# 44 adaLN pieces in the recurrence and the later ones in twos, in a hybrid RWKV-7 / RG-LRU trunk on one core

## The chip, the core and the metric

The kernel runs on one NeuronCore of a Trainium2 chip. A core has five engines with instruction queues of their own: TensorE (PE, matmuls into PSUM), VectorE (DVE), ScalarE (ACT), GpSimd (POOL) and SyncE (SP), which here issues nearly all transfers. The metric is device time in microseconds of one launch, the median of several runs.

## What is computed

One inference step of a two-layer trunk, width 2048, for a prompt of 256 rows and 8 single-row samples with carried state. Layer 0 mixes with RWKV-7, layer 1 with an RG-LRU; each mixer is followed by a causal ConvFFN of width 5632. The vectors that shift, scale and gate each stage (adaLN) come from the conditioning `c` through `w_mod`.

```python
mod = (silu(c) @ w_mod[i] + b_mod[i]).reshape(B, 6, 1, D)     # 2048 x 12288 for each layer
sh_m, sc_m, gt_m, sh_f, sc_f, gt_f = [mod[:, j] for j in range(6)]
h = rms_norm(x, g0) * (1 + sc_m) + sh_m
out = mixer(h)                       # RWKV-7: r, k, v, decay; scan over 256 rows of a 64 x 64 state, 32 heads
x = x + gt_m * rms_norm(out, g1)
h = rms_norm(x, g2) * (1 + sc_f) + sh_f
x = x + gt_f * rms_norm(conv_ffn(h), g3)
```

The scan is `S = S * d + (S a) b^T + v k^T`, `y = S r`, row by row; the outputs are `x` and all new states.

## The kernel before, in words

The work runs in stages: projections r, k, v (to about 395 us), the recurrence (to 763 us), the output projection of layer 0 (to about 875 us), the first ConvFFN (to about 1728 us), the RG-LRU (to about 2079 us), the second ConvFFN (to the end).

*Weights.* All large weights stream from `in_wst` as tiles of 128 x 2048 floats (1 MB), two groups of weights to a tile (class `Stream`, line 407). A group is split on ScalarE (`wh`, line 434) and VectorE (`wl`, line 435) into a high and a low half, and `mm_pieces` (448) spends 24 matmuls of 264 columns on it. `mm_group` (461) runs the groups of one set of four output tiles and asks for weights two tiles ahead.

*adaLN pieces.* `w_mod` beyond what the projections need comes as 160 pieces of 1 MB (`in_wmr`), 16 to a vector; a piece is four matmuls of 512 columns, each into 32 columns of the array (`wm_mm`, 342; the trace has 8 records to a piece). `wm_load` (372) loads one, `wm_pump` (377) computes the next in turn, and with `ahead` also loads the one behind it. The last piece of a vector is followed by a transposition and `mod_fin`. `mod` (399) hands out a vector and computes at once what is missing of it. `residual_and_h` (550) runs four pieces at its start (561), while the norm is waited for.

*Tiles.* Weights and pieces share five tiles of 1 MB in turn (`raw_tile`, 367): NRAW = 2 named `raw`, which live through the whole kernel, and three named `rawx`, of pools that are closed before the recurrence and opened behind it (lines 658, 871, 1426). In the recurrence there are only the `raw` tiles.

*The recurrence.* 16 pairs of heads go through jobs that are generators: load, prep, diag, solve, levels, prepb, seq (the scan by chunks of 64 rows), out, and the sample's own steps. The order in which their steps are written to the engines' queues is the table ORDER (37): `3p2` is three steps of prep for pair 2. `w` is a step of `pump_load` (1394), one half of a piece's transfer, and `u` is `pump_step` (1400), its matmuls. NPUMP = 60 pieces are done there; engines run in program order, with no reordering by the scheduler (line 1415). Elsewhere the tile scheduler orders the queues.

*Behind it.* `pace[0] = PACE` (1485) turns on a piece behind every fifth group of weights in `mm_group`. `out_proj` (1469) runs three sets of eight groups (the first set is written out above it), and in its first set the callback `bg_x` (1487) loads x back into U0 in four parts.

Of the kernel before, what the change touches and what calls it, by code (L numbers as in the profile page):

```python
# [38 lines left out]
l3 w1 p2 d0 3p2 4p1 a1 2b0 d1 b0 2b1 3g0 3p2 b1 p2 l5 p2 3p3 l3 2p3 2b0 d0 d1 s0 p3 w1 2p3 u0 u1 2p2 s2 3p3  # L39
5b1 p4 p3 2l4 g0 2p4 p5 s0 2p5 p4 3g0 l5 p5 w2 s0 w2 w3 2g0 p2 w3 g0 l6 p2 d2 p3 g0 5p2 6p3 d3 u2 u3 2g0 s0  # L40
3p4 2b2 w4 p4 3p5 b2 b1 4p4 b1 2p5 2b2 g0 s0 3b2 d2 d3 w4 2s2 5g0 p5 w5 3g0 2p4 u4 3p4 l7 p4 3b3 p5 2s2 s0 p5
2b3 g0 2b2 w5 u5 3b3 g0 p5 2w6 2p5 p4 2p5 p6 q0 2p6 2a0 2p5 u6 2a0 2q0 l6 s0 v0 b3 p6 2a0 5p6 b3 p6 s2 a0 p6
a0 3v0 2p7 a0 4h0 l8 l9 p7 l7 p7 d5 d4 l8 w7 2h0 3p7 4p8 v1 p7 v1 h0 2v1 l9 2p7 2v0 h0 p7 2p9 h0 p9 v1 s2 v1
p9 3v0 2v1 v0 v1 d4 d5 v1 2a1 p7 v0 q0 p6 w7 u7 2w8 u8 3s4 2a1 3q0 s2 2v2 q0 v1 w10 v2 3q0 p7 a1 p7 3q0 p7 2w9
v2 p6 l10 2q0 2p6 q0 2p6 s4 q0 2p6 a1 3p7 v3 3q0 v3 a0 s4 2a1 w10 v2 2p8 q0 2o0 q0 v3 v2 3b4 p8 a1 u9 u10 a1
p7 2p8 d6 3p8 l10 a2 p10 v3 o0 3p10 b5 o0 a2 q1 v3 2q1 d7 q1 2w11 o0 d6 q1 v3 s4 2a2 v2 d7 s4 v2 a2 a3 v2 w12
q0 2o0 s6 2p8 d8 2q1 v2 2o0 p8 a2 s4 3q1 o0 v2 p8 p9 s6 q1 l12 2q1 2a2 d8 q1 v3 q1 2p8 2a2 2p9 v3 4o0 3v3 3v4
q1 v4 3b4 a3 a2 b4 p8 b4 p9 3a3 w12 u11 u12 p9 v4 b4 3q1 2v4 a4 v4 b4 4q1 3a3 v4 h0 2s6 2w13 3p9 2b5 2p10 2b5
p10 2w14 b6 a3 2l11 3b5 a3 2v4 p10 p11 q1 a4 u13 u14 a3 2w15 b5 2o1 2w16 s6 a5 b5 3p9 p10 2q2 2a4 p9 q2 p9 d9
v5 2o1 a4 o1 2p11 2p9 o1 2v5 o1 s6 p11 s6 2q2 o1 u15 3q2 2w17 a4 2o1 a4 b7 d9 s8 3q2 2v5 a4 v5 2q2 a4 3q2 u16  # L50
4q2 s6 2w18 v5 q2 b6 p11 2q2 2p11 3v5 p11 3o2 3v6 3p10 v5 o1 b6 2p12 u17 u18 q3 p12 q3 a4 l12 p12 v6 a5 3p10
2q3 2l13 2b6 q3 o1 a4 q3 2b6 2w19 v6 2o2 w20 v6 s8 q3 a5 q3 p10 2q3 b6 q2 2o2 2p10 a5 w20 2a5 3v6 a6 u19 u20
p10 l14 o2 4q3 4a5 d10 2o2 w21 4q3 2v6 a5 2b6 q3 w21 2q3 p12 b7 q3 2p12 b7 o3 o2 o3 q4 s8 u21 d10 2o1 w22 2o2
w22 w23 u22 q4 q3 4p11 3q4 o2 p11 2a6 2q4 3p11 b8 4q4 2p11 2v7 w23 u23 2w24 2v7 d11 p13 2v7 a7 3p13 q3 p11 2q4
u24 2w25 w26 5q4 p12 w26 3v7 4s8 3q4 2a6 d11 2o3 l14 2q4 o4 p12 2v7 o3 u25 2o4 p12 2q5 2p12 q4 3a6 p12 2q5 w27
s10 w27 2a6 p12 d12 2p12 2b8 s14 a7 3p13 p12 a7 s8 4p14 2o3 q5 o3 o4 p13 u26 u27 q5 2p12 o4 v8 2l15 2o3 3v8 o3
d12 3q5 2b7 a7 2b7 3q5 2b8 q5 2a7 b8 4q5 b7 2w28 u28 o4 2p14 w29 b7 o3 q5 2o4 a7 b7 v8 b8 w29 o4 v8 o4 u29 3b8
v8 2q5 o4 a6 2a7 2w30 2v8 2s10 2o3 q5 v8 2q5 p13 v9 o5 2w31 a7 3p13 u30 a8 a7 u31 v8 o5 o4 5b9 a8 q6 a8 q5
2p13 3q6 a8 q6 2p13 2s10 b10 s10 p13 2b9 3a8 2w32 u32 q6 p15 2p14 p15 p14 p15 2w33 3o5 q6 p15 2w34 s10 d13 2q6
2o4 q6 u33 q6 w35 2q6 w35 b9 a8 v9 3q6 v9 2p13 v9 q6 2a8 2b9 q6 d13 2q6 v9 o5 2q6 p15 v9 o6 2p15 q6 a9 p15 o6  # L60
u34 u35 q7 o5 a8 p14 q7 2o5 2w36 w37 2p14 3q7 2o5 s10 p14 a9 p14 d14 p14 w37 4q7 v9 u36 w38 2v9 3a9 q7 p15 2v9
2a9 4q7 2b10 3q7 s12 4b10 w38 4q7 s12 2p14 3a9 2q7 a9 v10 u37 u38 a10 v11 2s12 v10 2p15 s12 p15 b11 p15 2v10
2p15 2w39 2p15 a11 4b11 v10 2b11 2v11 v10 2a10 3v10 v11 q6 q7 u39 2o6 s12 2o7 q8 d15 v10 4q8 v10 2w40 u40 2w41
2q8 a10 o5 s12 2o6 a10 2o6 o5 u41 5q8 w42 o5 w42 o6 2q8 o6 q8 o7 o6 o7 q8 u42 o7 p14 w43 q8 a10 2q8 a10 w43
3a10 v11 3q8 o8 q8 w44 o6 w44 o8 q9 v11 2o6 o7 4q9 2o8 2o7 q9 2a11 p14 a11 q9 u43 u44 d14 d15 o7 s12 v12 2q9
w45 o7 q9 w45 o8 2w46 o8 v12 4q9 3o8 2q9 o7 u45 3q9 v12 2w47 v12 o8 2v12 4q9 2o9 2s14 q10 o7 a11 2o7 o9 q10
s14 2q10 a10 q8 q10 2o9 b10 u46 2o8 3o9 2w48 u47 q10 b10 o9 q10 o9 b10 2q10 2b12 2q10 b12 3b11 4o9 o8 u48 2q10
b12 2q10 o8 q10 2b12 2w49 q9 b12 2a11 b12 2a11 q10 b13 3q10 2w50 b13 2q10 2s14 q10 2b12 2o10 u49 u50 a12 o10
q10 2o10 6b13 2a11 b14 w51 2b14 w51 4b14 a12 o10 u51 4o10 v13 2w53 2b13 3v11 3v12 a12 b14 3a12 v13 2p15 2v13
a12 2v11 v12 w52 v13 w52 q11 v13 u52 u53 2q11 v12 3a12 3q11 2a13 2b14 q11 v13 q11 s14 q11 v13 b15 q11 s14 q11  # L70
2v14 v13 a12 2o10 v14 w54 v14 v13 4a13 v14 w54 a13 v13 v14 w55 q11 w55 q11 u54 5q11 o10 3a13 q11 a13 2q11 b15
2q11 o10 2o11 q12 u55 2o11 q12 b15 2q12 o11 b15 v15 2q12 b15 2q12 2a14 b15 q12 2b15 a14 q12 2o11 2v15 4q12 v15
2o11 2w56 a14 q12 o11 3q12 q11 2v15 2a14 2q12 2b15 2q12 2o12 a14 q13 2q12 u56 2o11 2o12 o11 a14 2o12 o11 3q13
3o12 2q13 w57 o12 2a14 2q13 3o12 2q13 v14 2q13 o12 v14 2q13 v15 v14 q13 w59 2v15 2v14 a15 q13 4a15 2q13 2a15
w57 u57 3q13 a15 3q13 2o13 q14 v15 3q14 a15 v15 5q14 a15 3q14 o13 e0 o13 a15 10q14 o14 e0 o14 q14 4q15 o13
4q15 w58 6q15 o14 q15 e0 q15 w58 6q15 u58 e0 2o13 q15 2e0 q14 o14 o15 o14 e0 w59 u59 o15 2o13 2o14 4o13 o14
o13 6o14 a14 q15
# [1714 lines left out]
```

## Time and profile before

| | |
|---|---|
| median of 3 runs | 2910.57 us (2909.17 to 2916.7) |
| the profiled execution | 2907.63 us |
| its span, first to last instruction | 2905.9 us |
| TensorE busy | 2786.0 us, 96% |
| VectorE, ScalarE, GpSimd busy | 1756.3, 1366.6, 511.6 us |
| mean granted TensorE clock | 0.983 |
| moved by DMA | 648.48 MB, mean 223 GB/s |

The profile is one execution. Busy times are sums over stages with different limits, so the stretch of a stage is read for itself. Names of tiles are the program's, numbers of buffers are left out, and `L345` is line 345 of the kernel before; the changed kernel's lines are one less there.

### The profile page before, as it was taken

The page shows a single profiled execution, that of the slowest core. Times are in us where ns is not written, and L with a number is a line of the kernel's source. Part 1 is how long each engine was busy: PE and PEld are TensorE (multiplying, and loading weights), DVE is VectorE, ACT ScalarE, POOL GpSimd, SP SyncE. Part 2 cuts the span into 40 slices and gives each one's busy share as a digit, 9 for nine tenths or more (in the row PEclk, how much of TensorE's full clock was granted, in tenths as well). Part 3 has the DMA queues.
Part 4 walks back from the last instruction along what each step waited for, and adds up shares of the span by engine and source line. Part 5 has one row for each costly group of instructions (what it writes and reads, how often), then busy time and mean ns, then how long its engine had stood idle before and what let it go on. Part 6 is the DMA issues. An engine that isn't in the chain of part 4 may idle for free.

```text
span 2905.9 us, 61725 instructions
## 1 busy us (share of the span) xinstructions
PE 2786.0 (96%) x25868; PEld 2529.8 (87%) x25868; DVE 1756.3 (60%) x2830; ACT 1366.6 (47%) x2195; POOL 511.6 (18%) x1044
## 2 busy tenths in 40 slices
...
GB/s 329 285 264 257 171 162 230 286 269 250 209 248 214 234 242 229 235 234 231 233 235 229 242 258 188 220 231 221 261 221 236 231 176 181 182 177 186 174 188 77
DMA packets 148438, 648.48 MB, mean 223 GB/s; under 512 B 41360, under 2 KB 60960, under 8 KB 81600
## 3 DMA queue, kind: packets, MB, share of 16 engines
...
## 4 chain that ended last, share of the span: by engine, by line
PE 74%; DMA 4%; DVE 3%; ACT 2%; issue 1%; SPq 0%; POOL 0%; DVEq 0%; ACTq 0%; POOLq 0%
PE bk L455 16%; PE bk L456 15%; PE bk L457 15%; PE sq L455 6%; PE sq L456 6%; PE sq L457 6%; PE wm L345 5%; DMA raw<-in_wmr 3%; PE bk L895 1%; DVE bt L545 1%; ACT wh L434 0%; PE bk L901 0%; DVE U L546 0%; PE bk L582 0%; PE bk L1231 0%
## 5 line engine op out<-in xcount | busy, mean ns | idle before, releaser
L435 DVE TENSOR_TENSOR wl<-rawx,wh 128x1024 fp32r<-128x1024 f32 x460 | 565.4, 1231 | 488.2 <-ACT wh L434 468.5
L434 ACT CAST wh<-rawx 128x1024 fp32r<-128x1024 f32 x460 | 481.1, 1048 | 663.2 <-PE bk L456 454.2
L455 PE MATMUL bk<-AH,wh 128*128 128x264 f32 x2352 | 672.7, 286 | 0.0
L457 PE MATMUL bk<-AH,wl 128*128 128x264 f32 x2352 | 668.7, 284 | 0.2 <-DVE wl L435 0.2
L456 PE MATMUL bk<-AL,wh 128*128 128x264 f32 x2352 | 668.8, 284 | 0.0
L435 DVE TENSOR_TENSOR wl<-raw,wh 128x1024 fp32r<-128x1024 f32 x300 | 369.3, 1233 | 329.8 <-ACT wh L434 323.3
L455 PE MATMUL bk<-ah,wh 128*128 128x264 f32 x1822 | 525.7, 289 | 8.0 <-ACT ah L488 5.5
L457 PE MATMUL bk<-ah,wl 128*128 128x264 f32 x1822 | 520.8, 286 | 0.5 <-DVE wl L435 0.5
L456 PE MATMUL bk<-al,wh 128*128 128x264 f32 x1822 | 520.8, 286 | 0.0
L434 ACT CAST wh<-raw 128x1024 fp32r<-128x1024 f32 x300 | 313.7, 1048 | 434.8 <-PE bk L456 285.0
L455 PEld LDWEIGHTS bk<-AH,wh 128*128 128x128 f32 x2352 | 443.4, 189 | 34.4 <-issue 29.3
L456 PEld LDWEIGHTS bk<-AL,wh 128*128 128x128 f32 x2352 | 442.7, 188 | 0.2 <-DVE AL L489 0.2
L457 PEld LDWEIGHTS bk<-AH,wl 128*128 128x128 f32 x2352 | 441.8, 188 | 0.4 <-DVE wl L435 0.4
L455 PEld LDWEIGHTS bk<-ah,wh 128*128 128x128 f32 x1822 | 344.2, 189 | 33.9 <-issue 21.6
L457 PEld LDWEIGHTS bk<-ah,wl 128*128 128x128 f32 x1822 | 344.6, 189 | 1.4 <-DVE wl L435 0.8
L456 PEld LDWEIGHTS bk<-al,wh 128*128 128x128 f32 x1822 | 344.7, 189 | 0.6 <-DVE al L489 0.2
L455 PE MATMUL sq<-AH,wh 128*128 128x264 f32 x1040 | 297.3, 286 | 0.0
L456 PE MATMUL sq<-AL,wh 128*128 128x264 f32 x1040 | 295.7, 284 | 0.0
L457 PE MATMUL sq<-AH,wl 128*128 128x264 f32 x1040 | 295.4, 284 | 0.0
L1525 POOL COPY fgs<-gt 128x10 f32<-128x10 f32 x88 | 49.4, 585 | 1306.8 <-ACT gt L1519 1285.6
L455 PEld LDWEIGHTS sq<-AH,wh 128*128 128x128 f32 x1040 | 196.0, 189 | 15.2 <-issue 13.4
L456 PEld LDWEIGHTS sq<-AL,wh 128*128 128x128 f32 x1040 | 195.7, 188 | 0.0
...
## 6 DMA issues: line engine op xcount, KB each, us to landing
rawx<-in_wst SPq DMA_DIRECT2D x233, 1024.0 KB, 4.8
raw<-in_wst SPq DMA_DIRECT2D x151, 1024.0 KB, 4.9
raw<-in_wmr SPq DMA_DIRECT2D x120, 512.0 KB, 6.0
rawx<-in_wmr SPq DMA_DIRECT2D x57, 1024.0 KB, 6.5
raw<-in_wmr SPq DMA_DIRECT2D x43, 1024.0 KB, 5.1
rawx<-in_wmq SPq DMA_DIRECT2D x18, 1024.0 KB, 5.8
raw<-in_wmq SPq DMA_DIRECT2D x14, 1024.0 KB
...
```

The costliest lines, as they stand in the source:

```text
L345: PE.matmul(ps[32 * g:32 * g + 32, :cols], cs[:, k0 + kk, :], raw[:, (kk * 4 + g) * cols:(kk * 4 + g + 1) * cols], start=(k0 + kk == 0), s ...
L434: S.copy(wh, t)
L435: V.tensor_sub(wl, t, wh.bitcast(F32))
L455: PE.matmul(ps[:, :n], h[:, kk, sl], xh, start=first and kk == 0, stop=False)
L456: PE.matmul(ps[:, :n], h[:, kk, sl], xl, start=False, stop=False)
L457: PE.matmul(ps[:, :n], l[:, kk, sl], xh, start=False, stop=last and kk == 1)
L545: e.tensor_tensor(t, U1[:, j:j + n, :TP], r1[:, None, :TP].to_broadcast([128, n, TP]), op=mult)
L895: PE.matmul(out[HH[(i + turn) % 2]], lhs[HH[i]], rhs[HH[i]], start=start, stop=stop, skip_group_check=True)
L1525: G.tensor_copy(gs[:, m], gt[:, TP:])
```

## The change

PACE is 4 in place of 5, NRAW 3 in place of 2 (so three `raw` and two `rawx` tiles), NPUMP 44 in place of 60, and ORDER is another table: the same jobs for the 16 pairs, 16 `u` and 32 `w` fewer, in another order throughout. Behind the recurrence pieces come in twos: of each eight groups of weights, loads are written behind the fourth and fifth, and two pieces are computed behind the eighth, without loading ahead. The two loads ahead of a residual stage move from the fifth to the last group of their set. `bg_x` now runs over two sets of groups and loads a part of x at the second and seventh group of each.

```diff
-PACE = 5
-NRAW = 2
+PACE = 4
+NRAW = 3
-NPUMP = 60
+NPUMP = 44
 ORDER = """
-p0 s0 h0 g0 l0 p0 l0 3p0 g0 3p0 2l1 4p1 4p0 2g0 4p1 g0 3p1 p0 p1 b0 a0 4p0 l2 2p0 p2 b0 l2 2b0 2p1 w0 p1 b0 w0
+p0 p1 2g0 2l0 2p0 l1 p1 p0 s0 l1 p0 g0 3p0 l2 4p0 p1 l3 2p0 2w0 5p1 2p0 4p1 p2 3p0 p2 2g0 p3 p2 l2 p2 3p1 3b0
...
@@ mm_group
             if bg is not None:
                 bg(q)
-            if q == 4 and ahead:
+            pace[1] += 1
+            if pace[0]:
+                p = pace[1] % (2 * pace[0])
+                if p in (PACE, PACE + 1):
+                    wm_load(wm_state["i"] + p - PACE)
+                elif p == 0:
+                    wm_pump(2, False)
+            if ahead and q == nk // 2 - 1:
                 for w in range(ahead):
                     wm_load(wm_state["i"] + w)
-            pace[1] += 1
-            if pace[0] and pace[1] % pace[0] == 0:
-                wm_pump(1)
@@ out_proj
-            pss = pss0 if g == 0 and pss0 else mm_group(16, rhs, bg if g == bg0 else None, 2 if g == 3 else 0)
+            bgg = (lambda q: bg(q + 8 * (g - bg0))) if bg0 <= g < bg0 + 2 else None
+            pss = pss0 if g == 0 and pss0 else mm_group(16, rhs, bgg, 2 if g == 3 else 0)
@@ bg_x
-        if q in (3, 4, 5, 6):
-            SP.dma_start(U0[:, 4 * q - 12:4 * q - 8, 1:], I["xT"][:, 4 * q - 12:4 * q - 8])
+        if q % 8 in (1, 6):
+            j = 8 * (q // 8) + 4 * (q % 8 // 6)
+            SP.dma_start(U0[:, j:j + 4, 1:], I["xT"][:, j:j + 4])
```

Three places of the queues are spoken of below. The first is TensorE in the middle of the recurrence, about the ninth pair; before (`wm` is an adaLN piece, `x4` its four matmuls):

```order
L1203 MATMUL bk<-yl,cen 128x256
L895 MATMUL bk<-Vb,KQ 64x64 x2
L895 MATMUL bk<-St,AR 64x64 x2
L895 MATMUL yb<-KQ,Vb 64x64 x2
L895 MATMUL sq<-Vb,KQ 64x64 x2
L895 MATMUL yb<-AR,St 64x64 x2
L1231 MATMUL bk<-lw,lu_7662 128x256 x2
L895 MATMUL sq<-rb,E 64x64 x2
L895 MATMUL yb<-E,rb 64x64 x2
L345 MATMUL wm<-raw,cT 32x512 x4
```

and now:

```order
L904 MATMUL bk<-X_8033,ma 32x32 x16
L898 MATMUL sq<-rb,E 64x64 x2
L898 MATMUL yb<-E,rb 64x64 x2
L972 MATMUL bk<-lw,lu 128x256 x2
L974 MATMUL bk<-rn,e_112 128x256
L1053 MATMUL bk<-yh,blkr 128x256
L1054 MATMUL bk<-yl,blkr 128x256
L1213 MATMUL bk<-blk,gsq 128x2 x2
L344 MATMUL wm<-raw,cT 32x512 x8
```

Before, one piece stands here, the one before it 13 rows up; now two stand together, and the two before them are 27 rows up.

The second is TensorE at the end of the recurrence, just ahead of the output projection (`raw` with its number is the tile of a piece); before:

```order
L345 MATMUL wm_9408<-raw_10582,cT_72 32x512 x4
L1210 MATMUL bk_10648<-blk_108,gsq_10493 128x2 x2
L1390 MATMUL bk_10657<-ident_107,sy_5460 128x128
L1202 MATMUL bk_10663<-yh_10539,cen_113 128x256
L1203 MATMUL bk_10663<-yl_10540,cen_113 128x256
L345 MATMUL wm_9408<-raw_10367,cT_72 32x512 x4
L1219 MATMUL bk_10648<-ident_107,gsd_10651 64x128 x4
L1210 MATMUL bk_10683<-blk_108,gsq_10662 128x2 x2
L1231 MATMUL bk_10691<-lw_98,lu2_10485 128x256 x2
L1219 MATMUL bk_10683<-ident_107,gsd_10686 64x128 x4
```

and now:

```order
L1213 MATMUL bk_10526<-blk_108,gsq_10393 128x2 x2
L1205 MATMUL bk_10532<-yh_10404,cen_113 128x256
L1206 MATMUL bk_10532<-yl_10405,cen_113 128x256
L344 MATMUL wm_8646<-raw_10462,cT_72 32x512 x4
L344 MATMUL wm_8646<-raw_9971,cT_72 32x512 x4
L344 MATMUL wm_8646<-raw_9674,cT_72 32x512 x4
L1213 MATMUL bk_10557<-blk_108,gsq_10531 128x2 x2
L1222 MATMUL bk_10526<-ident_107,gsd_10555 64x128 x4
L1234 MATMUL bk_10571<-lw_98,lu2_10246 128x256 x2
```

Two pieces with the small matmuls of the `out` job between them have become three in a row, ahead of those matmuls.

The third is SP's queue at the start of the output projection (`in_xT` is x, `in_wmr` a piece, `in_wst` weights); before:

```order
L420 DMA rawx_11097<-in_wst 128x2048
L420 DMA rawx_11155<-in_wst 128x2048
L1489 DMA U0_78<-in_xT 128x4x264
L420 DMA rawx_11214<-in_wst 128x2048
L1489 DMA U0_78<-in_xT 128x4x264
L375 DMA raw_11249<-in_wmr 128x2048
L1489 DMA U0_78<-in_xT 128x4x264 x2
L420 DMA rawx_11363<-in_wst 128x2048
L375 DMA rawx_11425<-in_wmr 128x2048
```

and now:

```order
L419 DMA raw_10979<-in_wst 128x2048
L1494 DMA U0_78<-in_xT 128x4x264
L419 DMA rawx_11038<-in_wst 128x2048
L419 DMA rawx_11096<-in_wst 128x2048
L1494 DMA U0_78<-in_xT 128x4x264
L374 DMA raw_11126<-in_wmr 128x2048
L1494 DMA U0_78<-in_xT 128x4x264 x2
L419 DMA raw_11156<-in_wst 128x2048
L419 DMA rawx_11306<-in_wst 128x2048
```

The four loads of x stay close together; two loads of weights now stand between the first and the second.

## Rows read from the trace of the kernel before

**Rows 1.** The page: span, busy time by engine, and chain by line.
```profile
span 2905.9 us, 61725 instructions
...
PE 2786.0 (96%) x25868; PEld 2529.8 (87%) x25868; DVE 1756.3 (60%) x2830; ACT 1366.6 (47%) x2195; POOL 511.6 (18%) x1044
...
PE bk L455 16%; PE bk L456 15%; PE bk L457 15%; PE sq L455 6%; PE sq L456 6%; PE sq L457 6%; PE wm L345 5%; DMA raw<-in_wmr 3%; PE bk L895 1%; DVE bt L545 1%; ACT wh L434 0%; PE bk L901 0%; DVE U L546 0%; PE bk L582 0%; PE bk L1231 0%
```

**Rows 2.** Busy time by stretch: recurrence, its parts, x loads, second ConvFFN.
```profile
core 0: us, PE busy (x) PEld busy (x) DVE busy (x) ACT busy (x) POOL busy (x), PEclk, DMA share, GB/s
395.00:763.00 368.00, 316.50 (x5898) 199.44 (x5898) 227.98 (x538) 167.26 (x447) 148.63 (x349) 0.93 0.77 241
395.00:470.00 75.00, 56.43 (x701) 35.30 (x702) 53.35 (x140) 35.69 (x80) 30.03 (x73) 0.91 0.72 225
470.00:640.00 170.00, 153.11 (x3261) 98.00 (x3248) 112.50 (x247) 88.04 (x227) 91.03 (x221) 0.99 0.87 273
...
740.00:770.00 30.00, 24.10 (x287) 15.34 (x287) 12.60 (x41) 10.35 (x34) 1.74 (x3) 0.59 0.42 137
790.00:800.00 10.00, 10.00 (x85) 10.00 (x84) 5.11 (x9) 5.32 (x10) 1.08 (x2) 1.00 0.70 250
2400.00:2500.00 100.00, 100.00 (x822) 100.00 (x822) 54.77 (x74) 42.60 (x53) 6.25 (x18) 1.00 0.51 183
```

**Rows 3.** The same view of line 345 alone (PE, PEld, clock, DMA).
```profile
395.00:763.00 368.00, 94.42 (x480) 14.52 (x480) 0.93 0.77 241
```

**Rows 4.** Timeline of TensorE, 550 to 558 us: adaLN matmuls in the recurrence.
```profile
start us, us, engine line op out<-in xcount [idle before <-releaser]
...
551.04 1.05 PE L345 MATMUL wm<-raw,cT 128*32 128x512 f32 x4
553.61 1.05 PE L345 MATMUL wm<-raw,cT 128*32 128x512 f32 x4 [1.52 <-DMA raw<-in_wmr]
...
556.52 1.07 PE L345 MATMUL wm<-raw,cT 128*32 128x512 f32 x8
```

**Rows 5.** Waits of all engines, 380 to 765 us.
```profile
engine line waited for: us in total, times, longest us
PEld wm L345 <- DMA raw<-in_wmr: 54.5, 40, 5.2
...
ACT rb L935 <- PE bk L895: 28.2, 26, 3.7
ACT Sp L1183 <- DVE St L1178: 27.3, 19, 4.4
PE wm L345 <- DMA raw<-in_wmr: 24.4, 20, 4.3
```

**Rows 6.** DMA view of 395 to 763 us (packets; issues with time to landing).
```profile
DMA packets 60591, 88.87 MB, mean 241 GB/s; under 512 B 31888, under 2 KB 40464, under 8 KB 60016
...
raw<-in_wmr SPq DMA_DIRECT2D x120, 512.0 KB, 6.0
```

**Rows 7.** Chain that ended last, end of the recurrence (start, us, what).
```profile
755.05 1.86 PE wm L345 x8
758.60 1.87 PE wm L345 x8
760.47 1.05 PE bk L1219 x8
```

**Rows 8.** The same chain in the first ConvFFN: adaLN matmuls.
```profile
1015.30 1.00 PE wm L345 x8
1031.11 0.99 PE wm L345 x8
```

**Rows 9.** Timeline of TensorE, 2070 to 2115 us: three pieces on end.
```profile
2075.96 1.92 PE L345 MATMUL wm<-rawx,cT 128*32 128x512 f32 x16
2077.70 1.04 PE L345 MATMUL wm<-raw,cT 128*32 128x512 f32 x8
```

**Rows 10.** SP's queue in the first ConvFFN; landing time on the page.
```profile
1033.41 0.33 SPq L375 DMA_DIRECT2D raw<-in_wmr  x1
...
rawx<-in_wmr SPq DMA_DIRECT2D x57, 1024.0 KB, 6.5
```

More of the change, by code (lines that the diff above doesn't have):

```diff
@@ L37 @@
 ORDER = """
-p0 s0 h0 g0 l0 p0 l0 3p0 g0 3p0 2l1 4p1 4p0 2g0 4p1 g0 3p1 p0 p1 b0 a0 4p0 l2 2p0 p2 b0 l2 2b0 2p1 w0 p1 b0 w0
[L39 to L77, printed above, removed]
+p0 p1 2g0 2l0 2p0 l1 p1 p0 s0 l1 p0 g0 3p0 l2 4p0 p1 l3 2p0 2w0 5p1 2p0 4p1 p2 3p0 p2 2g0 p3 p2 l2 p2 3p1 3b0
@@ new lines @@
+p2 b1 p2 b0 2w1 b0 3p2 4p1 g0 b0 l3 l4 d1 p3 p2 l4 d0 b0 p2 2p3 2b1 w2 3b0 u0 w2 2p3 2p2 2p3 p4 p3 5p2 3p3 2p4
+a0 d0 g0 d1 p4 2g0 b2 p2 u1 3b1 2s0 p3 h0 p3 2g0 d2 2l5 2p3 u2 d3 b1 p5 2w3 s0 d2 g0 s0 4g0 w4 g0 2s0 d3 2p4
+2b1 2p3 b1 2p4 4b2 s2 p4 l6 p4 p3 2g0 2p4 w5 2p5 s2 4p5 3g0 4p4 b3 2p4 g0 2p5 u3 3p5 2g0 3b2 b3 p5 2b3 s0 p5
+g0 p5 b3 2p5 v0 3p6 2v0 w4 2v0 u4 l6 v1 q0 g0 p6 s2 2g0 a0 l7 p4 v0 p5 w6 v1 p5 s2 3a0 2s2 l7 2p6 a0 p6 2q0
+3p7 b2 2v1 w5 u5 2p7 b2 2p6 w6 u6 v0 p6 p7 2p6 2v1 2v0 2b3 2v0 4a0 b3 3h0 2b3 l8 b4 4p7 l8 h0 s2 p8 p7 s4 d5
@@ new lines @@
+2p8 h0 2q0 v1 d4 p8 q0 p9 v1 q0 l9 w7 s2 v2 3p7 4h0 2q0 3v1 q0 d4 3q0 l9 2q0 2p9 a1 p7 d5 2q0 p7 s6 p7 p9 6p6
+2p7 2q0 a1 2q0 b5 3v2 2q0 d7 2o0 l10 w8 b4 p6 v3 b4 q1 p8 l11 2v2 2q1 w8 q1 v3 2s4 3p8 2v2 v3 a1 w7 s4 q1 2p8
+v2 u7 o0 2s4 q1 v3 3q1 v2 q1 d6 2p8 q1 p9 w10 a0 v2 v3 o0 v3 a1 2w9 w10 2a1 2p9 3q1 s4 q1 3a1 2p8 l10 2q1 d6
+d7 3o0 s6 q1 o0 a1 u8 u9 2p10 p9 p8 2o0 2p10 3a2 u10 2b4 2a2 b4 a1 3q1 s4 v4 v3 b4 2v3 3a2 2q1 v5 p9 3v4 2v3
+2p8 3b5 2b4 2b5 p8 2p9 a2 p9 w12 2o0 v4 b5 b4 2w11 w12 b5 u11 u12 v4 s6 2b5 o0 2o1 l11 6q2 v4 q0 2w13 u13 o0
@@ new lines @@
+2v4 2a2 p8 s6 2v5 o1 3a3 2w15 2v4 w14 p9 v5 3q2 2p9 2q2 a3 2p9 a3 d8 p9 2s6 3q2 p10 p11 q2 w14 2o1 2p11 p10
+2q2 p9 q2 2v5 2p10 w16 2a3 3q2 o1 s10 d8 q2 s6 2a3 p11 q2 o2 2o1 u14 u15 o1 o2 p10 w16 2p10 q3 p10 v5 3q3 o2
+u16 2v5 a4 v5 p12 o1 v5 s6 v6 b6 2o2 q1 v6 d9 2q3 p11 a3 q3 2a4 b6 a3 p10 3q3 l12 v6 w17 a4 q2 2a4 v6 b6 q3 a4
+2b6 3q3 w17 4p10 a4 o1 b6 q3 v6 2b6 p10 l12 3q3 v6 q3 p11 s8 q3 b6 2q3 o3 2a4 o3 a5 q3 a5 w18 p10 w18 b6 2p12
+2o2 u17 b7 o2 l13 3q4 b7 p11 3p12 d9 2q4 w19 u18 b7 w19 d10 2o2 5p11 2w20 l13 a5 4q4 2v6 3v7 p12 v7 v6 a5 o2
```

23 lines of the change are left out of this document (added).

## The prediction

> **What bounds the kernel now.** I read the page first. Its busy lines and its chain of waits [rows 1] say that TensorE is busy 96% of the span, and that 3% of the chain is a wait for pieces of `in_wmr`. An average over stages does not say where these lie, so I went to the busy time by stretch [rows 2]. From 790 us on TensorE has no gap worth naming (10.00 of 10 us while the x loads run, 100.00 of 100 us in the second ConvFFN). The recurrence, 395 to 763 us, is different: TensorE is busy 316.5 of 368 us, VectorE 228, ScalarE 167, GpSimd 149, and the DMA engines 77%. In 470 to 640 us TensorE is at 153 of 170 us and DMA at 87%, so two resources are close to full there.
>
> What fills them is seen by restricting the same view to the line of the adaLN matmuls [rows 3]: 94.4 us of TensorE in 480 records, which is 60 pieces of 8 records, 1.57 us each. An undisturbed piece takes 1.07 us; one whose two halves land apart takes twice 1.05 us with a wait of 1.52 us between [rows 4]. The waits of the stretch [rows 5] name the same DMA: TensorE idle 24.4 us, its weight loads 54.5 us (partly beside running matmuls). Much of the other waiting is ScalarE for TensorE and VectorE (28.2 and 27.3 us), the latency of the state chain. The DMA view [rows 6] gives 88.87 MB at 241 GB/s, of which 120 half pieces of 512 KB are 63 MB.
>
> **The change, part by part.** The sum is made against the profiled execution, 2907.6 us. The median of the runs shown is 2910.6, so 2.9 us (0.1%) are added at the end. Up to the recurrence every engine but SP has the same instructions; SP loads into three tiles that live on and two that are closed, in place of two and three. Five tiles turn either way, so I cost it at nothing, with 3 us to either side.
>
> *Sixteen pieces leave the recurrence.* 16 x 1.57 = 25.1 us of TensorE [rows 3], and their part of the idle time before pieces, 16/60 of 24.4 = 6.5 us [rows 5].
>
> *A third tile and less traffic for the 44 that stay.* Before, a piece could load only when one of two tiles was free, that is after the last piece but one. What remains of the waits is 17.9 us, and of the halves that land apart 44 x (1.57 - 1.07) = 22.0 us. Without the 16 pieces the recurrence moves 88.9 - 16.8 = 72.1 MB, which at the 241 GB/s of [rows 6] takes 299 us where it took 368: loading has slack for the first time. The bounds are 0 (each wait returns, since the queue is shared with many small transfers) and 39.9 us. The order now sets pieces in twos, and the second of two then asks for data early again, so I take half, 20.0 us.
>
> *What the pieces covered.* In-order engines used a piece's time on TensorE to finish their steps; with it gone, the ScalarE waits of [rows 5] come to the front. The cost lies between 0 and all of 25.1 us; nothing in the rows says which, VectorE would rise from 62% to some 68%, and I take half, 12.6 us.
>
> *The end of the recurrence.* Three pieces now stand in a row where there were two with small matmuls between. There a piece takes 1.86 and 1.87 us and is on the chain [rows 7], at a granted clock of 0.59 on average [rows 2]. One more costs 1.9 us. Their second halves are loaded just ahead, behind other transfers on SP's queue, but so were those before.
>
> *Later pieces in twos.* In the ConvFFN a single piece stretches five groups of weights to 1031.11 - 1015.30 = 15.81 us [rows 8]. A group is 24 matmuls at 100/822 = 0.122 us [rows 2], five are 14.60 us, so a single piece costs 1.21 us. Two back to back start 1.74 us ahead of the third [rows 9], 0.87 us each. Before, 100 pieces came late: 12 ahead of the three residual stages, as now, 3 forced at 2076 us because a vector was not ready (2.6 us), and 85 single ones, 102.9 us. Now 116 come late: the 12, and 52 pairs at 1.21 + 0.87 = 2.08 us, 108.2 us. The difference is 2.7 us. No vector is forced: the 368 groups of weights up to there hold 46 pairs, so 44 + 92 + 8 = 144 pieces are done when the third residual stage asks for the ninth. Loads for a pair are written after the fourth and fifth group, 11.7 and 8.7 us ahead of use, and SP runs further ahead: it asked for a piece at 1033.41 and a piece takes 6.5 us to land [rows 10].
>
> The Trainium skill (TensorEngine Tiling (Array Packing), Key Properties) says that a change of tiling mode drains TensorE. The rows price that at 1.21 - 0.87 = 0.34 us a piece between full-width matmuls; if it held in the recurrence too, 16 x 0.34 = 5.4 us more would go, and the sum below would be 39.8 in place of 34.4 us. I leave it out, because the work around a piece there is in small tiles already and the waits show no idle time at pieces but for DMA.
>
> *x loads.* They are named at four points of two column groups, but on SP's queue they stay together: one more load of weights stands between the first and the second, the rest is as before. TensorE had no gap there, so nothing is gained, and I see no wait that takes its place.
>
> The sum: -25.1 - 6.5 - 20.0 + 12.6 + 1.9 + 2.7 = -34.4 us, 2873.2 us for a profiled execution, 2876 us for the median.
>
> **The rivals.** *All waits at pieces go and nothing takes their place*: -25.1 - 6.5 - 39.9 + 4.6 = -66.9 us, 2844 us. For it speaks the DMA slack, against it VectorE and the state chain.
>
> *The waits stay*: DMA at 87% in the middle keeps landings late and the third tile is filled by the next piece; -25.1 - 6.5 + 12.6 + 4.6 = -14.4 us, 2896 us.
>
> *The clock.* In 395 to 470 us, with TensorE busy 56 of 75 us, the granted clock was 0.91; in the middle it was 0.99; at the end, busy 24 of 30 us, 0.59 [rows 2]. So it falls where TensorE is less busy, and pieces are its longest work. At 0.91, 18% of a stretch is at 1.2 GHz. If the middle, then some 200 us long, came to that, 36 us would run at the lower level and give back up to half, 18 us: 2894 us. The Trainium skill (TensorE: Matmul & The Clock Gate, Part 1: The HAM clock gate) says that throttled is the default and activity releases it, which speaks for this one. Against it: the middle is denser, not emptier, if the waits go.
>
> *Cover lost whole and waits kept*: -25.1 - 6.5 + 25.1 + 4.6 = -1.9 us, 2909 us, no change.
>
> *Slower: pairs starve the stream.* A pair holds two of the five tiles, so weights run on three, and a late load stops TensorE in the ConvFFNs, where nothing covers it. It happens 52 times; 34.4 us of gain and 8.7 us of margin are gone at 43.1/52 = 0.83 us a pair. At the 1.52 us of [rows 4] it would be 79 us, 2955 us. Against it stands the lead of the loads above.
>
> **How the numbers follow.** A measurement can tell 0.3%, 8.7 us, from no change. The forecast with the inner half of its two open terms, 2860 to 2888 us, has 0.45; all waits gone 0.17 (below 2860); waits kept 0.15 and the clock 0.07 (2888 to 2902); no change 0.07; slower, by starved pairs or by one engine's queue held up by a step of the new order, 0.09. Faster is 0.84, same 0.07, slower 0.09. The range from 2846 to 2904 us leaves out the outer part of the best case and the slow ones.
>
> **What would show it.** Right: the recurrence some 35 to 40 us shorter, 352 records on the adaLN line there at less than 1.57 us a piece, DMA waits at pieces well under 18 us, pairs of 2.1 us every eight groups and no gap of TensorE beside them. Wrong: idle time between small matmuls that grows by more than the pieces gave, a clock under 0.95 in the middle, or `wl` waiting for `in_wst` in the ConvFFNs.

## The result and the profile after

The change takes 2869.82 us (median of 4 runs, 2867.66 to 2871.88) where the kernel before took 2910.88 (2909.17 to 2916.7): a ratio of 0.9855, 95% interval 0.9838 to 0.9872. The forecast was 2876. The profiled execution took 2867.66 us, 40 us less than the one of before, like the spans: 2865.9 against 2905.9 us.

The page of the changed kernel, span, busy time by engine, and the chain by line [rows 1]:

```profile
span 2865.9 us, 61683 instructions
...
PE 2756.3 (96%) x25868; PEld 2537.1 (89%) x25868; DVE 1760.4 (61%) x2830; ACT 1364.2 (48%) x2193; POOL 516.5 (18%) x1044
...
PE bk L454 18%; PE bk L455 17%; PE bk L456 17%; PE sq L454 7%; PE sq L455 7%; PE sq L456 7%; PE wm L344 5%; DVE wl L434 1%; PE bk L898 1%; DMA raw<-in_wmr 1%; ACT wh L433 1%; DMA rawx<-in_wst 1%; DVE bt L548 1%; PE sq L812 1%; POOL xs L1087 1%
```

TensorE is busy 29.7 us less, and `in_wmr` falls from 3% of the chain to 1%. Where the time went is told by the stretch from the end of the projections to the first matmul of the output projection. First the kernel before (whole, then its adaLN line alone; columns as in [rows 2, 3]):

```profile
397.50:770.90 373.40, 318.17 (x5895) 199.39 (x5893) 229.56 (x543) 171.14 (x455) 149.99 (x351) 0.93 0.77 243
397.50:770.90 373.40, 94.42 (x480) 14.52 (x480) 0.93 0.77 243
```

and the change:

```profile
397.50:728.00 330.50, 287.37 (x5768) 198.50 (x5767) 230.47 (x540) 169.23 (x455) 152.31 (x351) 0.92 0.73 226
397.50:728.00 330.50, 54.31 (x352) 9.85 (x352) 0.92 0.73 226
```

So this stretch gave 42.9 us. It splits into adaLN pieces 94.4 to 54.3 us (-40.1), other work of TensorE 318.17 - 94.42 = 223.8 to 233.1 us (+9.3), and idle time of TensorE 55.2 to 43.1 us (-12.1). A piece takes 54.31/44 = 1.23 us where it took 1.57.

Waits of TensorE and its weight loads, 395 to 722 us of the change [rows 5]:

```profile
PEld wm L344 <- issue: 13.1, 29, 2.6
...
PEld wm L344 <- DMA raw<-in_wmr: 5.8, 5, 3.1
```

```profile
PE wm L344 <- DMA raw<-in_wmr: 2.4, 2, 2.2
```

TensorE's 24.4 us of waiting for pieces are 2.4 us, the weight loads' 54.5 us are 5.8. The chain of waits, by line, says the same (before, 398 to 763 us; then the change, 398 to 722 us):

```profile
by line: DMA raw<-in_wmr 25.4%; PE wm L345 12.4%; PE bk L895 6.3%; PE bk L901 3.8%; issue 3.4%; PE sq L895 2.1%; PE bk L914 2.1%; PE bk L1231 2.1%; PE yb L895 1.9%; PE bk L1219 1.9%; DMA xc<-sx 1.7%; PE bk L1210 1.5%; DMA ss<-in_swkv 1.5%; 
```

```profile
by line: issue 13.0%; PE wm L344 7.7%; PE bk L898 7.3%; DMA raw<-in_wmr 7.1%; POOL xs L1087 4.4%; DVE smt L933 3.9%; POOL xtmp L1085 3.8%; DMA mb<-scr 3.2%; PE bk L904 3.1%; PE sq L898 3.0%; DVE cum L990 2.6%; PE bk L917 2.4%; PE bk L1146 2
```

At the end of the recurrence three pieces stand in a row, and then TensorE waits for weights (timeline of TensorE, 713 to 730 us of the change) [rows 7]:

```profile
713.36 1.01 PE L1213 MATMUL bk<-blk,gsq 128*128 128x2 f32 x4
...
714.94 4.56 PE L344 MATMUL wm<-raw,cT 128*32 128x512 f32 x24
719.43 0.61 PE L1213 MATMUL bk<-blk,gsq 128*128 128x2 f32 x4
...
728.06 0.59 PE L454 MATMUL bk<-ah,wh 128*128 128x264 f32 x1 [4.28 <-ACT wh L433]
```

SP's queue there (timeline of SP, same run) shows those weights asked for behind the last load of `lu2` (line 1200); the `raw` tiles that three of them go into hold pieces until TensorE is through with the last of them, at 719.5 us:

```profile
721.71 0.34 SPq L1200 DMA_DIRECT2D lu<-in_lup  x1
722.10 1.39 SPq L419 DMA_DIRECT2D raw<-in_wst  x3
```

The late pairs stand on the chain of the first ConvFFN every eight groups [rows 8]:

```profile
898.99 1.85 PE wm L344 x16
924.40 1.85 PE wm L344 x16
949.80 1.85 PE wm L344 x16
```

A turn of eight groups takes 25.40 us; 192 matmuls at 100/822 = 0.122 us (2400 to 2500 us has 822 of them, as before [rows 2]) are 23.4 us, so a pair costs about 2.0 us. From the first matmul of the output projection to the end of the span it is 2865.9 - 728.1 = 2137.8 us against 2905.9 - 770.9 = 2135.0 us before: 2.8 us more. The forecast's term was 2.7.

### The profile page after: what moved, and what is told of

It is laid out like the page before. It is cut to its first block, busy times and chain, and to the rows that moved or that the text cites. A ratio compares the mean times of both kernels' runs of the same rounds, so it can differ in the third digit from the quotient of the medians.

```text
span 2865.9 us, 61683 instructions
## 1 busy us (share of the span) xinstructions
PE 2756.3 (96%) x25868; PEld 2537.1 (89%) x25868; DVE 1760.4 (61%) x2830; ACT 1364.2 (48%) x2193; POOL 516.5 (18%) x1044
## 4 chain that ended last, share of the span: by engine, by line
PE 83%; DVE 6%; ACT 3%; DMA 3%; issue 2%; POOL 1%; SPq 0%; DVEq 0%; POOLq 0%; ACTq 0%
PE bk L454 18%; PE bk L455 17%; PE bk L456 17%; PE sq L454 7%; PE sq L455 7%; PE sq L456 7%; PE wm L344 5%; DVE wl L434 1%; PE bk L898 1%; DMA raw<-in_wmr 1%; ACT wh L433 1%; DMA rawx<-in_wst 1%; DVE bt L548 1%; PE sq L812 1%; POOL xs L1087 1%
## 5 line engine op out<-in xcount | busy, mean ns | idle before, releaser
L434 DVE TENSOR_TENSOR wl<-raw,wh 128x1024 fp32r<-128x1024 f32 x448 | 552.3, 1235 | 498.6 <-ACT wh L433 489.5
L433 ACT CAST wh<-raw 128x1024 fp32r<-128x1024 f32 x448 | 468.6, 1048 | 643.6 <-PE bk L455 430.0
L434 DVE TENSOR_TENSOR wl<-rawx,wh 128x1024 fp32r<-128x1024 f32 x312 | 381.6, 1225 | 331.7 <-ACT wh L433 326.6
L433 ACT CAST wh<-rawx 128x1024 fp32r<-128x1024 f32 x312 | 326.5, 1048 | 457.8 <-PE bk L455 337.4
```

The source lines that it names most:

```text
L433: S.copy(wh, t)
L434: V.tensor_sub(wl, t, wh.bitcast(F32))
```

## The experiments

Theory A is the prediction's own: the gain comes from fewer pieces and a third tile. Its rival B: it comes from the new order of steps. The first four runs take the parts of the change one at a time.

**Fewer pieces alone.** The old ORDER without 16 of its 60 pieces (the 4th, 8th, 12th and 15th of each 15), two tiles, later pieces in twos as in the change:

```diff
-PACE = 5
+PACE = 4
-NPUMP = 60
+NPUMP = 44
```

> The order of before with 16 of its 60 pieces taken out (evenly), two tiles as before, later pieces in twos. Theory A (what counts is the pieces: their time on TensorE and the waits at them): 25.1 + 6.5 us less in the recurrence, about half of 25.1 given back as lost cover, 2.7 us more late: some 16 to 24 us faster than before, and the 44 pieces left still wait for their data, 10 us or more of TensorE's idle time. Rival B (the new order does it): within 8 us of before.

Measured: 2904.7 us (2896.8 to 2916.4), ratio 0.9972 (0.9956 to 0.9987).

**The third tile alone.** The kernel before with one number changed:

```diff
-NRAW = 2
+NRAW = 3
```

> The kernel before with three tiles that live on, and nothing else: 60 pieces, old order, single pieces late. Theory A: the third tile takes half or more of the 24.4 us of idle time and of the 0.5 us by which a piece with split halves is longer, 15 to 27 us faster. Rival C (DMA is full in the middle, so a third tile only waits earlier): within 8 us of before, the waits at the pieces still above 20 us.

Measured: 2906.6 us (2903.2 to 2913.4), ratio 0.998 (0.9967 to 0.9992).

**Both, in the old order.** The first run with `NRAW = 3`.

> The order of before without 16 pieces, three tiles, later pieces in twos; it differs from the change in the order of steps (and the x loads) alone. Theory A: 30 to 38 us faster than before, so within 8 us of the change. Rival B (the new order is worth half of the gain or more): 20 us faster at most, 20 us slower than the change.

Measured: 2901.0 us (2893.0 to 2904.4), ratio 0.9964 (0.995 to 0.9978). The three give 0.3, 0.2 and 0.4%; the change gave 1.45%. So the parts on which the prediction put its terms bring some 10 of the 41 us, and the order of steps the other 30. The waits of this run show why (395 to 748 us):

```profile
PEld wm L342 <- DMA raw<-in_wmr: 32.6, 21, 4.7
...
PE wm L342 <- DMA raw<-in_wmr: 16.7, 14, 3.8
```

With a third tile and 44 pieces the data still come late. A free tile does not bring them; the load stands where the table puts it, median 16 steps ahead of the matmuls for the second half in the old order, 34.5 in the new one.

**Single late pieces.** The changed kernel with one piece behind every fourth group, loaded one ahead, in place of two behind the eighth:

```diff
-                p = pace[1] % (2 * pace[0])
-                if p in (PACE, PACE + 1):
-                    wm_load(wm_state["i"] + p - PACE)
-                elif p == 0:
-                    wm_pump(2, False)
+                if pace[1] % pace[0] == 0:
+                    wm_pump(1)
```

> The change with single pieces behind every fourth group in place of two behind every eighth. Theory A (each turn between full-width matmuls and a piece costs 0.34 us): 52 turns more, 17 to 18 us slower than the change, the recurrence as it is in the change. Rival D (pairs hold two tiles and cost the stream as much as they save): no difference above 5 us.

Measured: 2884.5 us (2883.2 to 2888.4), 14.7 us over the change, ratio to before 0.9911 (0.9893 to 0.9929). Over 52 pairs that is 0.28 us a pair saved, beside the 0.34 us that the prediction priced from rows for a change between full-width and 32-column matmuls. So twos pay for most of the 16 pieces that moved, 16 x 1.21 = 19.4 us if they came singly.

**Old order, early loads of pieces.** If the lead of the loads is what the new order has, it can be given to the old one. The run with both, its 88 half loads written 50 and 37 steps ahead of the matmuls (median), nothing else moved:

```diff
-p0 s0 h0 g0 l0 p0 l0 3p0 g0 3p0 2l1 4p1 4p0 2g0 4p1 g0 3p1 p0 p1 b0 a0 4p0 l2 2p0 p2 b0 l2 2b0 2p1 w0 p1 b0 w0
+p0 s0 h0 g0 l0 p0 l0 3p0 g0 3p0 2l1 4p1 4p0 2g0 4p1 g0 3p1 p0 p1 b0 a0 4p0 l2 2p0 p2 b0 l2 b0 w0 b0 w1 3p1 b0 l3
...
```

> Old order of the other steps, 44 pieces, three tiles and the later pieces in twos, as in the run with both (2901.0 us, recurrence up to the first matmul of the output projection 355.5 us), but the loads of each piece are moved up in the table: the first half 50 steps and the second 37 steps ahead of its matmuls (median 26 and 16 before, 46 and 34.5 in the change). Theory A, the gain of the new order is the lead of its loads: the waits of TensorE for pieces fall from 16.7 us to under 5, a piece falls from 1.54 to about 1.25 us (13 us), and the recurrence shortens by 15 to 25 us, total 2876 to 2886. Theory B, the gain lies in the order of the other steps: the waits go as well, but other waits take their place; the recurrence shortens by under 8 us, total 2893 to 2903. Theory C, loads asked for early stand in SP's queue behind a tile that is not free and hold up the pairs' own loads: no gain or a loss, 2900 to 2915.

Measured: 2902.2 us (2897.4 to 2907.6), ratio 0.9963 (0.9949 to 0.9977): no gain over the run with both. TensorE's waits (395 to 762 us) say where it went:

```profile
PE bk L917 <- DMA vj<-Vd: 16.3, 6, 5.3
...
PE bk L1251 <- DMA raw<-in_lups: 7.0, 2, 3.5
...
PE bk L972 <- DMA lu<-in_lup: 5.2, 1, 5.2
```

The wait for pieces is down to 1.2 us; the pairs' own small loads now come late, behind the pieces' on the queue that they share, which is what theory C said. The wait changed its name.

**New order, late loads of pieces.** The mirror, 29 and 17 steps:

```diff
-p2 b1 p2 b0 2w1 b0 3p2 4p1 g0 b0 l3 l4 d1 p3 p2 l4 d0 b0 p2 2p3 2b1 w2 3b0 u0 w2 2p3 2p2 2p3 p4 p3 5p2 3p3 2p4
+p2 b0 w0 b0 3p2 4p1 g0 b0 w0 l3 l4 d1 p3 p2 l4 d0 b0 p2 2p3 2b1 3b0 u0 p3 w1 p3 2p2 2p3 p4 p3 3p2 w1 2p2 3p3 p4
...
```

> The mirror: the changed kernel with the loads of each piece moved down to 29 and 17 steps ahead of its matmuls, about where they were before; nothing else. Theory A (lead of the loads): DMA waits at pieces return (10 us or more of TensorE), a piece rises from 1.23 to about 1.5 us, the recurrence grows by 15 to 25 us, total 2885 to 2895. Theory B (order of the other steps): grows by under 8 us, total 2870 to 2878, although some waits return. Theory C: unchanged or a little faster, 2865 to 2872.

Measured: 2903.6 us (2899.9 to 2908.6), ratio 0.9966 (0.9954 to 0.9978): 34 us of the 41 are gone, more than theory A gave it. It is also more than the waits themselves, 20.8 us where the change has 2.4. TensorE waits for pieces again (395 to 759 us):

```profile
PE wm L344 <- DMA raw<-in_wmr: 20.8, 16, 3.4
```

**No pieces at all**, in either order (NPUMP = 0, no `u` and `w` in the table). All of w_mod's later work is left to the stages behind, so only the recurrence is read.

```diff
-NPUMP = 44
+NPUMP = 0
```

> The changed kernel without any piece in the recurrence (no loads, no matmuls of w_mod there; they come all at once behind it, so that only the stretch up to the first matmul of the output projection is read, 330.3 us in the change). What remains is the order of the other steps. Theory A: the new order owes its gain to the loads, so its floor without pieces and that of the old order are alike within 6 us. Theory B: this floor lies 15 us or more below that of the old order. In both, TensorE is then under 78% busy, and the 44 pieces at 1.23 us (54 us of work) cost less than 54 us on the path: I expect 295 to 310 us.

> The old order, three tiles, without any piece in the recurrence, read in the same stretch (355.5 us with 44 pieces, 373.4 us before with 60). Theory A: 295 to 312 us, within 6 us of the new order's floor. Theory B: 315 to 335 us, 15 us or more above it. If the floor were as high as 345 us, pieces would hardly cost anything in the old order and fewer pieces could not have helped.

Same stretch, new order and then old order:

```profile
397.50:728.10 330.60, 269.20 (x5423) 213.01 (x5421) 226.25 (x536) 169.28 (x455) 150.92 (x351) 0.82 0.32 87
```

```profile
397.50:737.50 340.00, 266.58 (x5433) 214.92 (x5431) 232.76 (x538) 169.74 (x455) 153.64 (x352) 0.81 0.31 85
```

I had expected 295 to 312 us. The new order takes 330.6 us without pieces and 330.5 with 44 of them; the old one takes 340.0 without. So the 44 pieces cost the new order about nothing, while the old order pays 33.4 us for its 60 (373.4). At most 9.4 us of the gain is the order of the other steps and loads (one execution of each; in the old order's, TensorE waits 7.8 us for the small load vj, in the new one's not at all); the rest is that pieces are free in the new order. They are free in a way I had not seen: without them TensorE's other work takes 269.2 us in place of 233.1, at a granted clock of 0.82 in place of 0.92 over the stretch.

**Old order, all loads early.** The pairs' loads moved up too: kj 31 steps ahead of use, vj 53, lu 45 (medians).

```diff
-p0 s0 h0 g0 l0 p0 l0 3p0 g0 3p0 2l1 4p1 4p0 2g0 4p1 g0 3p1 p0 p1 b0 a0 4p0 l2 2p0 p2 b0 l2 b0 w0 b0 w1 3p1 b0 l3
+l0 l1 l0 l1 p0 s0 h0 g0 4p0 g0 3p0 l2 2p1 b0 2p1 4p0 2g0 4p1 l2 g0 3p1 p0 p1 a0 p0 l3 5p0 p2 3b0 p1 w0 p1 w1 p1
...
```

> The run with the old order and early piece loads (2902.2 us) lost its waits for pieces, but TensorE then waited 16.3 us for vj, 5.2 for lu, and VectorE 10.4 for kj: the pairs' own small loads came late behind the pieces. Here these are moved up as well: kj 31 steps ahead of its use (median; 8 there, 19 in the change), vj 53 (35 there, 50.5 in the change), lu 45; every other step stays in the old order, 44 pieces, three tiles, later pieces in twos. Theory A2, what the new order gives is lead for all loads that share the queue, the pieces' and the pairs': these waits fall under 8 us in sum and the recurrence shortens by 15 us or more, total 2870 to 2888. Theory B2, the old order of the compute steps is itself at its limit (its floor without pieces is 9 us above the new one's) and other waits take over: total 2893 to 2904.

Measured: 2906.6 us (2903.1 to 2914.2), ratio 0.9989 (0.9977 to 1.0001). The waits for vj and kj are gone, that for pieces is 3.2 us, and the sample's loads are the late ones (395 to 762 us):

```profile
PE bk L1251 <- DMA raw<-in_lups: 17.1, 4, 7.3
```

Twice loads were moved up in this table and twice nothing came of it. That speaks for theory B2, but not cleanly: the total lies above B2's range too, and one load was late here as well. `in_lups` goes into the same `raw` tiles as the pieces (line 1246 of the changed kernel).

**The last three pieces early.** A try at a faster kernel: pieces 41 to 43 out of the tail, 95 to 195 steps up, and two tiles of the output projection's weights asked for in the tail.

```diff
-4q15 e0 4q15 w41 q15 e0 7q15 h0 e0 q15 2e0 5q15 w41 o13 q15 o14 o15 w42 u41 u42 w43 u43 o14 o15 o13 o14 2o13
-2o14 5o13 6o14 q15 q14 a15 a14
+7q14 v15 6q14 2v15 3a15 q14 x0 3q14 a15 e0 o13 v15 2q14 o14 e0 2o14 o13 2v15 q14 4q15 e0 5q15 e0 7q15 h0 e0 q15
+2e0 5q15 o13 q15 o14 o15 o14 o15 o13 o14 2o13 2o14 5o13 6o14 q15 q14 a15 a14
...
+    def wst_ahead():
+        ws.limit = NPC
+        for n in range(2):
+            ws.load_to(ws.i // 2 + n)
+            yield
```

> The changed kernel with its last three pieces taken out of the tail: their matmuls, three in a row at 715 us (4.5 us at a granted clock of about 0.57 and on the chain), move some 95 to 195 steps up, their loads with them, and the first two tiles of weights of the output projection are asked for from the two tiles that come free, 40 to 80 steps ahead of the end, in place of behind the last lu load (TensorE waits 4.3 us for them at 728 us). If both are on the path: first matmul of the output projection at 720 to 723 us in place of 728.1, total 2861 to 2866 against 2869.8. Rival: the end of the recurrence is the chain of the last pair's steps on ScalarE and VectorE, the pieces only fill its gaps, and the weights are not late by more than the split waits anyway: within 2 us of the change, 2868 to 2872.

Measured: 2873.4 us (2872.6 to 2876.0), ratio 0.9868 (0.9853 to 0.9882): 3.6 us slower than the change, if anything, and above both expectations. Here `x` is a step of `wst_ahead`. The wait for weights shrank from 4.3 to 2.4 us, but the first matmul of the output projection starts at 734.2 us, not at 720 to 723. Up to 680 us the two traces run within some 0.2 us of each other (the pieces of 672.74 us in the change start at 672.90 here). The three pieces now stand at 682.55, 688.75 and 693.93 us, and the step that stands ahead of the three in the change, L1213 at 713.36 us, comes 7.8 us later (L1212 here):

```profile
672.90 3.13 PE L343 MATMUL wm<-raw,cT 128*32 128x512 f32 x16
...
721.12 1.01 PE L1212 MATMUL bk<-blk,gsq 128*128 128x2 f32 x4
```

So the loss is made where the pieces now stand. From that step to the first matmul of the output projection this kernel takes 13.1 us where the change takes 14.7, no more than the 1.9 us by which the wait for weights shrank: 4.56 us of pieces less did not shorten the tail. The stretches 710 to 730 us of this run:

```profile
710.00:715.00 5.00, 5.00 (x74) 3.48 (x65) 2.51 (x10) 2.44 (x8) 0.00 (x0) 0.50 0.41 157
715.00:720.00 5.00, 4.13 (x79) 2.90 (x79) 2.67 (x10) 1.67 (x7) 0.00 (x0) 0.50 0.00 0
720.00:725.00 5.00, 3.98 (x41) 3.36 (x38) 0.94 (x5) 1.62 (x7) 0.00 (x0) 0.50 0.06 13
725.00:730.00 5.00, 5.00 (x23) 3.33 (x20) 1.42 (x4) 1.35 (x3) 0.64 (x2) 0.50 0.52 167
```

and of the change:

```profile
710.00:715.00 5.00, 4.50 (x63) 3.44 (x67) 1.79 (x7) 1.24 (x5) 0.00 (x0) 0.50 0.34 130
715.00:720.00 5.00, 5.00 (x31) 1.49 (x30) 0.60 (x2) 0.97 (x4) 0.00 (x0) 0.64 0.36 121
720.00:725.00 5.00, 3.78 (x27) 2.44 (x26) 2.27 (x7) 3.21 (x9) 1.37 (x2) 1.00 0.48 128
```

The third column from the right is the granted clock. In the change it is at the lower level (1.2 GHz) from 710 us until near the end of the three pieces, and at the upper one behind them; L1213, four matmuls, takes 1.01 us ahead of them and 0.61 behind. Without the pieces the clock stays at the lower level to the end of the tail, and the same four matmuls take 1.01 us both times.

**Loads of x in their old place.**

```diff
-        if q % 8 in (1, 6):
-            j = 8 * (q // 8) + 4 * (q % 8 // 6)
-            SP.dma_start(U0[:, j:j + 4, 1:], I["xT"][:, j:j + 4])
+        if q in (3, 4, 5, 6):
+            SP.dma_start(U0[:, 4 * q - 12:4 * q - 8, 1:], I["xT"][:, 4 * q - 12:4 * q - 8])
```

> The changed kernel with the four loads of x back at the fourth to seventh group of the first set of the output projection. TensorE had no gap there before or after, so all theories expect no difference that can be measured: 2867 to 2873 us. If the spread of these loads had a part in the gain, it would be some us slower and TensorE would wait for weights between 765 and 800 us.

Measured: 2871.7 us (2864.8 to 2872.4), ratio 0.9853 (0.9834 to 0.9871): no difference, as expected.

**Pieces evenly spread.** The new order of all other steps, but a piece every 34 of them (the change has gaps from 1 to 137 steps), loads 47 and 36 steps ahead:

```diff
-a0 d0 g0 d1 p4 2g0 b2 p2 u1 3b1 2s0 p3 h0 p3 2g0 d2 2l5 2p3 u2 d3 b1 p5 2w3 s0 d2 g0 s0 4g0 w4 g0 2s0 d3 2p4
+a0 d0 g0 w2 d1 p4 2g0 b2 p2 3b1 s0 w2 u1 s0 p3 h0 p3 2g0 d2 2l5 2p3 d3 b1 p5 s0 d2 g0 s0 3g0 w3 2g0 2s0 d3 2p4
...
```

> The changed kernel with every step of the recurrence but the pieces in its place; the first 41 pieces stand evenly, one every 34 other steps (single, where the change sets many in twos or close together and leaves gaps of up to 137 steps), their halves loaded 47 and 36 steps ahead; the three at the tail stay. Theory P, where the pieces stand is part of the gain (the change puts them where TensorE would wait for ScalarE and VectorE, so that 44 pieces cost nothing on the path): here they push the chain of the state back, the recurrence grows from 330 us by 10 us or more, total 2880 to 2895, without long waits for pieces. Theory Q, the order of the other steps and loads that are early enough are all there is: 2867 to 2875. If waits of TensorE for pieces return (over 10 us), the run tells of lead and not of place.

Measured: 2901.8 us (2894.6 to 2906.4), ratio 0.996 (0.9949 to 0.9971): 32 us slower than the change and above theory P's range, with no wait of TensorE for a piece among its rows. The same stretch, whole and for the adaLN line:

```profile
397.50:754.50 357.00, 298.86 (x5779) 205.29 (x5777) 228.48 (x542) 169.76 (x455) 152.65 (x351) 0.88 0.68 210
397.50:754.50 357.00, 54.28 (x352) 8.06 (x352) 0.88 0.68 210
```

The pieces themselves cost the same to 0.03 us. What is longer by 26.5 us is idle time, 58.1 against 43.1 us (+15.0), and TensorE's other work, 244.6 against 233.1 us (+11.5), at a granted clock of 0.88 against 0.92. But not all of it is place. The tile of the sample's loads came later, 11.0 us of TensorE's waits where the change has 5.6:

```profile
PE bk L1251 <- DMA raw<-in_lups: 11.0, 2, 8.4
```

Both waits lie early (at 437 and 473 us): the step at 478 us of the change is reached at 488.1 us here. Behind it TensorE waits for no load in this run until the weights at the end, which are as late in both (4.3 and 4.5 us). The rest of the stretch, first the change and then this run, is still 16.4 us longer:

```profile
478.00:728.00 250.00, 225.03 (x4817) 156.05 (x4815) 172.41 (x392) 128.84 (x362) 117.89 (x266) 0.94 0.72 226
488.10:754.50 266.40, 231.90 (x4828) 161.64 (x4820) 171.94 (x392) 129.53 (x362) 119.41 (x272) 0.89 0.66 204
```

Ten pairs of pieces that stand together in the change stand singly here; ten more turns between matmul shapes, at the 0.28 to 0.34 us found behind the recurrence, would be some 3 us (an estimate, not measured here). So theory P holds: where the pieces stand is worth some 16 us in the part where TensorE waits for no load, and up to 32 us together with what the places of their loads do to other loads.

All these runs side by side, from the same two views of each (stretch from 397.5 us to the first matmul of the output projection, in us; the profiled executions of the runs with both and with even pieces were the fastest of theirs, 8 and 7 us below their medians; the projections end between 396.7 and 401.3 us, so up to 3.8 us of a row are theirs). The change's recurrence was run again in the kernels with single late pieces and with the old x loads: they reach that matmul at 732.5 and 732.3 us where the change does at 728.1, so rows within some 4 us are not told apart:

| recurrence | stretch | pieces | other work | idle | clock |
|---|---|---|---|---|---|
| before, 60 pieces | 373.4 | 94.4 | 223.8 | 55.2 | 0.93 |
| old order, 44, third tile | 355.6 | 67.6 | 229.5 | 58.5 | 0.91 |
| the same, early loads | 370.4 | 56.2 | 246.9 | 67.3 | 0.87 |
| the same, all loads early | 369.5 | 58.7 | 243.7 | 67.1 | 0.87 |
| old order, no pieces | 340.0 | 0 | 266.6 | 73.4 | 0.81 |
| the change | 330.5 | 54.3 | 233.1 | 43.1 | 0.92 |
| late loads | 367.4 | 64.5 | 239.1 | 63.8 | 0.90 |
| pieces evenly spread | 357.0 | 54.3 | 244.6 | 58.1 | 0.88 |
| new order, no pieces | 330.6 | 0 | 269.2 | 61.4 | 0.82 |

Other work and clock go together down the table: 224 to 233 us at 0.91 to 0.93, 239 at 0.90, 244 to 247 at 0.87 and 0.88, 267 to 269 at 0.81 and 0.82, for the same matmuls. The product of the two stays within 208 to 221 us in all rows, so an order at a lower clock pays for it in the work itself, beside its gaps. Idle time alone does not tell the clock: 58.5 us of it stand beside 0.91, 58.1 beside 0.88.

## Why the prediction was right, and where not

*The sum and its ledger.* The forecast of 2876 us was 6 us high. By entries of the profile its terms were each of the right sign and each too small, and the errors partly cancel. Pieces on TensorE: -25.1 and, of the 20.0, half of 22.0 for halves that land together, -36.1; measured -40.1. Waits for pieces: -6.5 and half of 17.9, -15.5; measured 24.4 to 2.4, -22.0. What takes their place, lost cover and tail: +14.5; measured, as other work (+9.3) and other idle time (-12.1 + 22.0 = +9.9), +19.2. Together -37.1 forecast, -42.9 measured. That the total came out near is in part luck: the causes that these terms were put down to do not give them.

*The step that failed is what the terms were put down to.* "Sixteen pieces leave the recurrence" at 16 x 1.57 us, and "a third tile and less traffic": done by themselves in the old order these two give 10 us of the 41, not 51.6 less cover. The price of a piece is not its time on TensorE: it is 33.4/60 = 0.56 us on the path before, about nothing in the change, and 26.4/44 = 0.6 us when spread evenly through the changed table, a part of this being other loads that came late. The order of steps has no term in the sum, and it carries some three quarters of the result: 31 us lie between the run with both parts in the old order and the change. Its parts overlap, since late loads of pieces alone give back 34 us, and even places 32. The one sentence on it (it "now sets pieces in twos") was read from one place of the queue: by the traces 30 of 60 pieces stood in twos on TensorE before, and now 20 of 44 do and three in a row. The rival "the waits stay", 2896 us, describes what happens without the new order: 2901 us measured.

*The bandwidth argument.* 72.1 MB at 241 GB/s as slack for the loads was true and not the point. The waits stayed at 16.7 us with that slack in the old order, where the second half of a piece is asked for 16 steps (median) ahead of its use; moved up to 37 steps, the pieces' loads left the others late (vj 16.3 us).

*The end of the recurrence.* The third piece was to cost 1.9 us. Three pieces take 4.56 us there, 1.52 each in place of 1.86, but the clock behind them is at its upper level, and the tail without them took as long but for the wait for weights: their cost there is about nothing. That wait grew from 2.45 to 4.28 us, which I had not named: the loads stand behind the last load of `lu2`.

*The clock.* As a rival (2894 us) it did not come in the change: 470 to 640 us went from 0.99 to 0.95 (row below), which is at the bound that I had set, and the stretch as a whole from 0.93 to 0.92. As a mechanism it was the right one to name: in the evenly spread run and in both early-load runs the clock is 0.87 to 0.88 and TensorE's other work longer by 11 us and more. The Trainium skill (TensorE: Matmul & The Clock Gate, Part 1: The HAM clock gate) has throttled as the default and activity as what lifts it; the trace agrees, 0.82 with no pieces against 0.92 with them.

```profile
470.00:640.00 170.00, 154.34 (x3331) 107.22 (x3327) 115.19 (x259) 93.36 (x245) 91.47 (x225) 0.95 0.80 253
```

*Later pieces, x loads, starving.* The 2.7 us for pieces in twos came as 2.8 us in all behind the recurrence, which is luck too: TensorE's waits for late pieces grew there by 5.5 us (1.3 to 6.8), so all the rest came out some 5 us below the forecast, the pairs at 2.0 us in place of 2.08 among it. The turn between matmul shapes was priced at 0.34 us a pair and measured at 0.28. The Trainium skill (TensorEngine Tiling (Array Packing), Key Properties) has a rule that a change of tiling mode drains TensorE; the 0.28 us agree with it, though the trace shows a cost and no drain, and no run here prices it inside the recurrence. Waits for weights behind the first matmul of the output projection are 2.4 us in all (0.6 before), so the slower rival had no ground. The waits are the thing that I missed: the last of the pieces at a residual stage now waits 2.67, 2.57 and 1.57 us for its data (840, 1697 and 2048 us), where a pair and the stage's own four pieces meet, as in this row of the changed kernel's TensorE timeline:

```profile
840.35 1.06 PE L344 MATMUL wm<-raw,cT 128*32 128x512 f32 x8 [2.67 <-DMA raw<-in_wmr]
```

The x loads cost and gave nothing that can be measured.

What stays open: why the old order gains nothing when nearly all its waits at pieces are gone. Its floor without pieces is only 9.4 us higher. Other loads were late in both runs with early loads (vj 16.3 us, `in_lups` 17.1 us), and the even spread shows that the place of pieces can cost 16 us where TensorE waits for no load, so I take both for the cause; this is not shown, since the new places were not tried in the old table.
